# Encoder layer: four AdaLN columns on TensorE, a shorter first norm, last additions on GpSimd and TensorE, sixteen output places

## The chip, the cores and the metric

One NeuronCore of a Trainium2 chip. It has a matrix engine (TensorE: PE for products, PEld for loading their weights), a vector engine (VectorE: DVE), a scalar engine (ScalarE: ACT), a general one (GpSimd: POOL), and queues that issue DMAs (here SyncE's, SP, and a few at the end on ACT's). Products accumulate in PSUM, eight banks of 128 x 512 f32; everything else works in SBUF. The metric is the device time of one execution in microseconds.

## What is computed

One layer of an encoder on 2048 tokens of width 1024, all f32: windowed attention, then a SwiGLU feed-forward net, each with a norm before and after and with shift, scale and gate from a conditioning vector c (AdaLN).

```python
c_act = jax.nn.silu(c)
mod = (c_act @ ada_w[i] + ada_b[i])[:, None, :]
sh1, sc1, g1, sh2, sc2, g2 = jnp.split(mod, 6, axis=-1)
h = rmsnorm(x, mix_norm_pre[i]) * (1.0 + sc1) + sh1
y = windowed_gqa_sink(h, att_w_qkv[j], att_w_o[j], att_sink[j], rel_bias)
x = x + g1 * rmsnorm(y, mix_norm_post[i])
h = rmsnorm(x, ffn_norm_pre[i]) * (1.0 + sc2) + sh2
y = swiglu(h, ffn_w_in[i], ffn_w_out[i])
x = x + g2 * rmsnorm(y, ffn_norm_post[i])

def rmsnorm(x, g):
    y = xf * lax.rsqrt(jnp.mean(xf * xf, axis=-1, keepdims=True) + EPS)
    return (y * g).astype(x.dtype)
```

mod has 6 x 1024 entries. In the kernel an entry stands on a partition, so mod is 48 columns of 128: columns 0 to 7 are the first shift (sh1), 8 to 15 the first scale (sc1), and so on.

## The kernel before, in words

Activations are kept transposed: width on partitions, in KT = 8 tiles of 128, and tokens along the row, in four chunks of CH = 512. An f32 product is made of three: each operand is split into a rounded part `hi` (ACT writes it as a cast) and a rest `lo` (a subtraction on DVE or POOL), and `three` multiplies hi by hi, hi by lo and lo by hi at the fast rate. A product of two plain f32 operands, as the sums of squares against `ones`, is one call and two records in the profile.

The kernel does not run in the order in which it is written. A recorder takes down every operation, and a planner of its own (`forward`, `backward`, `schedule`) sets the order per engine from assumed costs (`cost`) and from times at which each operation is due; an addition or a scaling given to POOL may be moved to DVE. So every instruction bears one line of the helper that emits it (L748), and what names a place is the tile. Engines and queues work their lists in order. A tile's place in SBUF or PSUM is taken again when its last reader is through.

The parts that the change touches:

- **The start (chunk 0).** SP loads the eight tiles `x` of chunk 0, then c, the AdaLN weights `ada` (512 KB for a column of mod) and the projection weights `wqkv` (448 KB for a row of tiles) in turn, through five places `raws`. `squares0` squares the x tiles on ACT and adds them in pairs on DVE; `rstd_of` multiplies the sums by `ones` on PE, which leaves the mean on every partition, and makes of it a first value of the inverse root on ACT (Ln, Exp) and one Newton step (a square on ACT, three operations on DVE). `ada_reduce` multiplies a tile of ada_w by silu(c), `cb`, and sums the row on DVE: one column of mod. `Chunk.h(k)` scales x by the norm (DVE), applies scale and shift (ACT) and splits the result.
- **The first wave.** For each k, seven output tiles of the projection get their three products with `hi`, `lo` of tile k: 8 groups of 21 products, into seven PSUM banks. Afterwards come the other five output tiles, with weights `w1` (the second part of a row of wqkv, 320 KB).
- **The output projection of the attention** (`OProj.fill`): its result `y` of a chunk, eight tiles, has twelve places (four in the last chunk).
- **The end.** The last part of the feed-forward net's second product is done plainly for chunks 2 and 3, chunk 3 in two halves of 256 columns: per output tile twelve products (`gls`, `wl`), an addition into `z` on DVE, a square on ACT, an addition into `zacc` on DVE. When a section's eight tiles are through, `rstd_out` makes its norm and `finish` writes z * norm, then * gate + x (two DVE operations), and a DMA stores it. In the last half the eight squares `zsl` go to PE one by one as eight sums.

## Time and profile before

| | |
|---|---|
| Median of three runs | 2037.0 us (2036.87 to 2037.06) |
| The profiled execution | 2036.67 us, its span 2034.9 us |
| Granted clock of TensorE, mean | 0.995 |
| Busy: PE, PEld, DVE, ACT, POOL | 1991.0, 1659.3, 1703.6, 1069.9, 554.4 us |
| PE's idle time | 43.9 us of the span |
| DMA | 415.23 MB, mean 204 GB/s |

A row of a timeline is the start, the duration, the engine, the source line, the operation, its tiles and shapes, how many, and in brackets how long the engine was idle before and what released it. Durations of products overlap, so their rate is read from the distance of starts. Groups give the total and the mean duration in ns of one instruction. A row of stretches gives busy time and instructions of each engine between two times.

### The profile page before, as it was taken

To read this page: it belongs to the slowest core of one execution; us is meant where nothing else is said; L and a number is where in the kernel's file an instruction comes from. 1 tells how busy PE (TensorE), PEld (TensorE's weight loads), DVE (VectorE), ACT (ScalarE), POOL (GpSimd) and SP (SyncE) were. 2 spreads that over 40 slices of the span, in tenths; PEclk is the share of its full clock that TensorE was granted. 3 is DMA by queue.
4 is the path that set the end of the run, shared out by engine and by line. 5 is a ranking of instruction groups with operands and counts; after the bars stand their busy time and mean duration, and the time that the engine had idled before them with its cause. 6 is when DMAs were issued, how large, how long until landed. Compare 5 with 4: busy or idle time off the path is not lost.

```text
span 2034.9 us, 28945 instructions
## 1 busy us (share of the span) xinstructions
PE 1991.0 (98%) x9366; PEld 1659.3 (82%) x9366; DVE 1703.6 (84%) x3075; ACT 1069.9 (53%) x2094; POOL 554.4 (27%) x501
## 2 busy tenths in 40 slices
PE   5999999999999999999999999999999999999997
PEld 4888888888787778788888888888888888888886
DVE  7868888877989888988787998776776789989998
ACT  5557766777778864344343533333333744455432
POOL 1302342344657513432333221111111000120031
PEclk9999999999999999999999999999999999999999
DMA  8896765576787694444446743333233694398543
GB/s 308 303 324 211 241 210 173 192 279 229 253 279 251 226 361 150 160 161 166 165 160 242 272 155 130 119 135 104 83 124 105 240 334 144 117 326 297 173 154 109
DMA packets 208580, 415.23 MB, mean 204 GB/s; under 512 B 19963, under 2 KB 61996, under 8 KB 205356
## 3 DMA queue, kind: packets, MB, share of 16 engines
q1 hardware_dynamic: 207852, 412.84, 58.7%
q8 instruction: 75, 1.23, 0.2%
q14 instruction: 77, 0.63, 0.1%
q10 hardware_dynamic: 576, 0.52, 0.1%
HBM read 278.52 MB, written 134.77 MB: 203 GB/s over the span
## 4 chain that ended last, share of the span: by engine, by line
PE 91%; DVE 5%; DMA 2%; issue 1%; ACT 1%; SPq 0%; POOL 0%; DVEq 0%; ACTq 0%; POOLq 0%
PE bank L748 91%; DVE z L748 1%; DVE ada L748 1%; DVE zx L748 1%; DVE pr L748 0%; DMA o_d<-of 0%; DMA ly<-y_d 0%; DMA x<-xT 0%; DMA ol<-o_d 0%; SPq L748 0%; DVE u_i L748 0%; DMA ada<-ada_w 0%; DVE x L748 0%; DVE plo L748 0%; DVE ws_i L748 0%
## 5 line engine op out<-in xcount | busy, mean ns | idle before, releaser
L748 PE MATMUL bank<-ht,ws_i 128*128 128x512 f32 x1584 | 374.0, 389 | 0.0
L748 PEld LDWEIGHTS bank<-ht,ws_i 128*128 128x128 f32 x1584 | 297.3, 188 | 61.7
L748 PE MATMUL bank<-hb,wa_i 128*128 128x512 f32 x1056 | 254.2, 389 | 0.4 <-DVE hb L748 0.4
L748 PEld LDWEIGHTS bank<-hb,wa_i 128*128 128x128 f32 x1056 | 198.1, 188 | 42.0 <-DVE hb L748 0.7
L748 PE MATMUL bank<-ol,wo 128*128 128x512 f32 x768 | 206.1, 396 | 2.3 <-ACT yacc L748 1.1
L748 DVE TENSOR_TENSOR u_i<-bank,u_i 128x512 f32<-128x512 f32 x176 | 120.9, 688 | 80.0 <-PE bank L748 77.8
L748 ACT CAST ws_i<-s_i 128x512 fp32r<-128x512 f32 x132 | 81.9, 620 | 192.2 <-DVE s_i L748 96.2
L748 ACT ACTIVATE pr<-pr,nm 128x385 f32<-128x385 f32 (+1 forms) x256 | 154.8, 606 | 53.3 <-DVE nm L748 47.4
L748 DVE CUSTOM_DVE_ANT_0 pr<-bank,bias,nsink 128x384 f32<-128x384 f32 (+1 forms) x256 | 149.9, 594 | 25.6 <-PE bank L748 22.0
L748 PEld LDWEIGHTS bank<-ol,wo 128*128 128x128 f32 x768 | 141.2, 188 | 28.7 <-ACT yacc L748 1.5
L748 POOL TENSOR_SCALAR pr<-pr,rs 128x384 f32<-128x384 f32 (+1 forms) x177 | 114.7, 660 | 179.7 <-DVE rs L748 168.3
L748 POOL TENSOR_TENSOR p_i<-p_i,u_i 128x512 f32<-128x512 f32 x41 | 66.9, 1632 | 344.6 <-DVE u_i L748 173.9
L748 POOL TENSOR_TENSOR z<-z,z 128x512 f32<-128x512 f32 x29 | 45.4, 1577 | 345.9 <-ACT ws_o L748 264.4
L748 PE MATMUL bank<-k,q 128*128 128x384 f32 (+1 forms) x512 | 135.5, 345 | 1.5 <-DVE nm L748 1.5
L748 PE MATMUL bank<-hi,ws 128*128 128x512 f32 x384 | 134.3, 400 | 0.0
L748 DVE TENSOR_TENSOR plo<-bank,phi 128x512 fp32r<-128x512 f32 x184 | 120.8, 684 | 9.8 <-ACT phi L748 8.7
L748 PE MATMUL bank<-hb,ws_i 128*128 128x512 f32 x528 | 127.1, 390 | 1.8 <-ACT p_i L748 1.8
L748 ACT CAST wa_i<-wiri 128x512 fp32r<-128x512 f32 x132 | 81.3, 620 | 90.1 <-PE bank L748 78.4
L748 PE MATMUL bank<-ht,wa_i 128*128 128x512 f32 x528 | 126.8, 389 | 0.0
L748 DVE TENSOR_TENSOR wa_i<-wiri,wa_i 128x512 fp32r<-128x512 f32 x132 | 103.4, 784 | 19.0 <-ACT wa_i L748 19.0
L748 PEld LDWEIGHTS bank<-hb,ws_i 128*128 128x128 f32 x528 | 98.9, 188 | 23.2 <-ACT p_i L748 2.6
L748 DVE TENSOR_TENSOR z<-bank,z 128x512 f32<-128x512 f32 (+1 forms) x164 | 107.7, 659 | 11.4 <-PE bank L748 10.2
(261 smaller groups left out, 4422.6 us busy)
## 6 DMA issues: line engine op xcount, KB each, us to landing
wiri<-w_in SPq DMA_DIRECT2D x88, 512.0 KB, 4.6
ada<-ada_w SPq DMA_DIRECT2D x40, 512.0 KB, 5.1
q_d<-e SPq DMA_DIRECT2D x32, 512.0 KB, 4.4
q<-q_d SPq DMA_DIRECT2D x16, 1024.0 KB, 7.0
wo<-wo_d SPq DMA_DIRECT2D x16, 1024.0 KB, 6.0
wiro<-w_out SPq DMA_DIRECT2D x40, 384.0 KB, 5.0
g_d_b<-p_i SPq DMA_DIRECT2D x44, 256.0 KB, 3.3
g_d_t<-p_i SPq DMA_DIRECT2D x40, 256.0 KB, 2.0
```

The source lines that it names most:

```text
L748: o.ins = getattr(engs[o.eng], o.fn)(*args, **kw)
```

## The change

**AdaLN columns on TensorE.** Columns 8, 0, 9 and 1 of mod, which groups 0 and 1 need, come from PE: `ct` holds silu(c) as 128 x 8, `ada_t` holds ada_w in the orientation of a product, and `ada_products` makes eight products of 128x128 weights with one column of ct, summed in one column of a PSUM bank; DVE adds the bias. DVE's reductions of these four columns go (52 instead of 56 in all). The silu of the long `cb` now comes later.

**Norm and split at the start.** `squares0` leaves four sums instead of three with one addition less. For chunk 0, `rstd_of(short=True)` replaces the square on ACT and three DVE operations by three DVE operations. `Chunk.h` of chunk 0 writes `hi` by its own activation, next to that of x, instead of a cast of x. `WARM` = 14 products of `ones` with itself are put first on PE; nothing reads them.

**Places and splits.** AdaLN tiles of the start get ten places of their own (`raws0`) whose space w2 takes afterwards. The lo parts of the first part of wqkv go to DVE alone.

**The end.** The norm's last operation writes to PSUM (`keep`), z is scaled in one operation by gate and norm (`scaled`), and x is added on POOL (`finish_apart`; the planner leaves four to DVE). Squares are added on POOL where the planner keeps them there. In the last half, pairs of squares are added before PE sums them (five sums instead of eight), and x + z is made on PE by products with the identity, copied by ACT.

**Sixteen places** for y of the output projection instead of twelve.

The planner lays the whole order anew; its cost of a plain f32 product gets a floor of 230 ns.

```diff
+ADA_PE = 2
+WARM = 14
...
-                op.occ, op.lat = 860 * n // CH, 1060 * n // CH
+                op.occ, op.lat = max(860 * n // CH, 230), max(1060 * n // CH, 400)
...
-    def rstd_of(alloc, psp, ptag, acc, tag, r=None, direct=False):
+    def rstd_of(alloc, psp, ptag, acc, tag, r=None, direct=False, short=False, keep=False):
...
         act.activation(r, ps, AF.Ln, bias=epsc)
         act.activation(r, r, AF.Exp, scale=-0.5)
+        if short:
+            dve.scalar_tensor_tensor(t, ps, EPS, r, ALU.add, ALU.mult)
+            dve.scalar_tensor_tensor(t, t, -0.5, r, ALU.mult, ALU.mult)
+            out = ps if keep else r
+            dve.scalar_tensor_tensor(out, t, 1.5, r, ALU.add, ALU.mult)
+            return out
...
-            dve.tensor_tensor(sq[6], sq[4], sq[6], ALU.add)
-            self.acc = [sq[0], sq[2], sq[6]]
+            self.acc = sq[::2]
...
-            act.activation(xt, xt, AF.Identity, bias=mod[:, k:k + 1], scale=coef[:, 0, k:k + 1])
...
+            if c == 0:
+                act.activation(hi, xt, AF.Identity, bias=mod[:, k:k + 1], scale=coef[:, 0, k:k + 1])
+            act.activation(xt, xt, AF.Identity, bias=mod[:, k:k + 1], scale=coef[:, 0, k:k + 1])
+            if c == 0:
+                return scaled, dve.tensor_tensor(lo, xt, f(hi), ALU.subtract)
...
+        raws0 = open_pool(first, "raws0", KT * C2 * 2 // D, side="right")
...
+        sp.dma_start(ct, a["ct"])
         sp.dma_start(cb, row(a["c"], D))
...
+        def ada_products(k):
+
+            for e, t in enumerate((8 + k, k)):
+                w = raws0.tile([P, D], F32, tag="raw", name=f"adat{t}")
+                sp.dma_start(w, a["ada_t"][t])
+                j = 2 * k + e
+                for i in range(KT):
+                    pe.matmul(ada_ps[:, j:j + 1], w[:, i * P:(i + 1) * P], ct[:, i:i + 1],
+                              start=i == 0, stop=i == KT - 1)
+                dve.tensor_tensor(mod[:, t:t + 1], ada_ps[:, j:j + 1], adab[:, t:t + 1], ALU.add)
...
-            split(t[:, 0], t[:, 1], w[:, :n], pool)
+            split(t[:, 0], t[:, 1], w[:, :n], pool if i else dve)
...
+        for _ in range(WARM):
+            pe.matmul(warm[:, :P], f(ones), f(ones), start=True, stop=True)
...
-            ada_reduce(*ada_load(8 + k, raws))
-            ada_reduce(*ada_load(k, raws))
+            if k < ADA_PE:
+                ada_products(k)
+            else:
+                ada_reduce(*ada_load(8 + k, raws0))
+                ada_reduce(*ada_load(k, raws0))
...
-                y = yp.tile([P, CH], F32, tag="y", name=f"y{c}_{n}", bufs=4 if c == NCH - 1 else 12)
+                y = yp.tile([P, CH], F32, tag="y", name=f"y{c}_{n}", bufs=4 if c == NCH - 1 else 16)
...
+    def scaled(c, k, r, cols):
+        y = ys[c, k][:, cols]
+        dve.scalar_tensor_tensor(y, y, coef[:, 3, k:k + 1], r, ALU.mult, ALU.mult)
+        return y
+
+    def finish_apart(c, k, r, cols):
+        y, xr = scaled(c, k, r, cols), late_x[c, k][:, cols]
+        pool.tensor_tensor(xr, xr, y, ALU.add)
+        sp.dma_start(out[c, :, k, cols], xr)
...
-                square(c, n, cols, dve)
+                square(c, n, cols, pool)
...
+                if n % 2 and n < KT - 2:
+                    pool.tensor_tensor(sq[n - 1], sq[n - 1], sq.pop(n), ALU.add)
...
-    r = rstd_out(*prev, lsq)
+    r = rstd_out(*prev, list(sq.values()), keep=True)
+    c, cols = prev
     for k in range(KT):
-        finish(prev[0], k, r, late_x[prev[0], k], prev[1], (dve, dve))
+        xr = late_x[c, k][:, cols]
+        ps = psC.tile([P, CH], F32, tag="p", name=f"px{k}")[:, cols]
+        pe.matmul(ps, ident, xr, start=True, stop=False)
+        y = scaled(c, k, r, cols)
+        pe.matmul(ps, ident, y, start=False, stop=True)
+        act.copy(xr, ps)
+        (act if k % 2 else sp).dma_start(out[c, :, k, cols], xr)
```

What stands in a row now, at three places. A name's first number is left out; its last one only counts tiles.

**PE from its first instruction**, before (sums of squares, then group 0 of the first wave):

```order
L748 MATMUL bank<-nsq_0_86,ones 128x512
L748 MATMUL bank<-nsq_2_95,ones 128x512
L748 MATMUL bank<-nsq_6_115,ones 128x512
L748 MATMUL bank<-hi_0_164,w_0_137 128x512 x7
L748 MATMUL bank<-lo_0_176,w_0_137 128x512
L748 MATMUL bank<-hi_0_164,w_0_137 128x512
```

and after:

```order
L756 MATMUL bank<-ones 128x128 x14
L756 MATMUL bank<-nsq_0_103,ones 128x512
L756 MATMUL bank<-nsq_2_113,ones 128x512
L756 MATMUL bank<-nsq_4_122,ones 128x512
L756 MATMUL bank<-nsq_6_132,ones 128x512
L756 MATMUL bank<-ct,adat_105 128x1 x8
L756 MATMUL bank<-ct,adat_111 128x1 x8
L756 MATMUL bank<-ct,adat_120 128x1 x8
L756 MATMUL bank<-ct,adat_125 128x1 x7
L756 MATMUL bank<-hi_0_199,w_0_168 128x512 x7
L756 MATMUL bank<-lo_0_216,w_0_168 128x512
L756 MATMUL bank<-hi_0_199,w_0_168 128x512
```

The products with `ct` (one column each) stand between the sums and group 0; the eighth of the last tile comes twelve products later.

**DVE at the same place**, from the last addition of squares to the norm's last operation, before:

```order
L748 TENSOR_TENSOR nsq_6_115<-nsq_4_105,nsq_6_115 128x512
L748 ISA ada_93,mod<-ada_93,cb,adab 128x1024
L748 ISA mod 128x1
L748 ISA ada_98,mod<-ada_98,cb,adab 128x1024
L748 ISA mod 128x1
L748 TENSOR_TENSOR w_0_137<-wqkv_0_103,w_0_137 128x896
L748 SCALAR_TENSOR_TENSOR nta_143<-bank,nta_143 128x512
L748 ISA ada_113,mod<-ada_113,cb,adab 128x1024
L748 ISA mod 128x1
L748 TENSOR_SCALAR nta_143<-nta_143 128x512
L748 SCALAR_TENSOR_TENSOR coef<-mod,gains 128x1
L748 TENSOR_TENSOR nr_129<-nr_129,nta_143 128x512
```

and after, to the first `lo`:

```order
L756 TENSOR_TENSOR nsq_6_132<-nsq_6_132,nsq_7_137 128x512
L756 TENSOR_TENSOR mod<-bank,adab 128x1
L756 SCALAR_TENSOR_TENSOR nta_170<-bank,nr_148 128x512
L756 SCALAR_TENSOR_TENSOR nta_170<-nta_170,nr_148 128x512
L756 TENSOR_TENSOR mod<-bank,adab 128x1
L756 SCALAR_TENSOR_TENSOR nr_148<-nta_170,nr_148 128x512
L756 SCALAR_TENSOR_TENSOR coef<-mod,gains 128x1
L756 TENSOR_TENSOR x_0_71<-x_0_71,nr_148 128x512
L756 TENSOR_TENSOR w_0_168<-wqkv_0_115,w_0_168 128x896
L756 TENSOR_TENSOR x_1_75<-x_1_75,nr_148 128x512
L756 TENSOR_TENSOR mod<-bank,adab 128x1
L756 TENSOR_TENSOR lo_0_216<-x_0_71,hi_0_199 128x512
```

The reductions (`ISA ada`, with the readout `ISA mod`) are gone from ahead of the norm; two additions of one column take their place, and the second stands ahead of the norm's last operation.

**DVE around the lo tile of group 5**, before:

```order
L748 ISA ada_286,mod<-ada_286,cb,adab 128x1024
L748 ISA mod 128x1
L748 SCALAR_TENSOR_TENSOR coef<-mod,gains 128x1
L748 ISA ada_255,mod<-ada_255,cb,adab 128x1024
L748 ISA mod 128x1
L748 TENSOR_TENSOR lo_4_359<-x_4_76,hi_4_331 128x512
L748 ISA ada_300,mod<-ada_300,cb,adab 128x1024
L748 ISA mod 128x1
L748 TENSOR_TENSOR lo_5_371<-x_5_78,hi_5_357 128x512
```

and after:

```order
L756 ISA ada_244,mod<-ada_244,cb,adab 128x1024
L756 ISA mod 128x1
L756 ISA ada_254,mod<-ada_254,cb,adab 128x1024
L756 ISA mod 128x1
L756 SCALAR_TENSOR_TENSOR coef<-mod,gains 128x1
L756 TENSOR_TENSOR w_5_370<-wqkv_0_266,w_5_370 128x896
L756 ISA ada_280,mod<-ada_280,cb,adab 128x1024
L756 ISA mod 128x1
L756 TENSOR_TENSOR lo_5_416<-x_5_90,hi_5_397 128x512
```

Now a group's two reductions, its coef and the weights' lo come in a row, and before lo of group 5 (`lo_5`) stands one reduction of group 6.

**The end.** PE after the products of the last output tile, before:

```order
L748 MATMUL bank<-gls_3_17735,wl_17915 128x256 x3
L748 MATMUL bank<-zsl_18263,ones 128x256 x2
L748 MATMUL bank<-zsl_18273,ones 128x256 x2
L748 MATMUL bank<-zsl_18283,ones 128x256 x2
L748 MATMUL bank<-zsl_18295,ones 128x256 x2
```

after (`zsl` are the squares, `zx` the x tiles, `z` the scaled results):

```order
L756 MATMUL bank<-zsl_18233,ones 128x256
L756 MATMUL bank<-zsl_18266,ones 128x256
L756 MATMUL bank<-zsl_18292,ones 128x256
L756 MATMUL bank<-zsl_18346,ones 128x256 x2
L756 MATMUL bank<-zx_0_17857,ident 128x256
L756 MATMUL bank<-zx_1_17878,ident 128x256
L756 MATMUL bank<-zx_2_17892,ident 128x256
L756 MATMUL bank<-zx_3_18223,ident 128x256
L756 MATMUL bank<-zx_4_18250,ident 128x256
L756 MATMUL bank<-zx_5_18281,ident 128x256
L756 MATMUL bank<-z_0_6_16505,ident 128x256
L756 MATMUL bank<-z_1_6_16606,ident 128x256
```

POOL's last instructions were, before:

```order
L748 TENSOR_TENSOR z_1_4_16504<-z_1_4_16504,z_1_3_16487 128x512
L748 TENSOR_TENSOR z_2_6_16915<-z_2_6_16915,z_2_1_16608 128x512
L748 TENSOR_TENSOR z_2_4_16782<-z_2_4_16782,z_2_3_16709 128x512
L748 TENSOR_TENSOR z_3_6_16963<-z_3_6_16963,z_3_1_16643 128x512
L748 TENSOR_TENSOR z_3_4_16824<-z_3_4_16824,z_3_3_16741 128x512
```

and are, at the place that feeds PE's sum of `zacc_18076` (chunk 3's first half), after:

```order
L756 TENSOR_TENSOR zacc_17927<-zacc_17927,zsq_5_0_18028 128x512
L756 TENSOR_TENSOR zacc_18076<-zacc_18076,zsq_3_0_18130 128x256
L756 TENSOR_TENSOR zacc_18076<-zacc_18076,zsq_4_0_18142 128x256
L756 TENSOR_TENSOR zx_0_17724<-zx_0_17724,z_0_2_16407 128x512
L756 TENSOR_TENSOR zacc_18076<-zacc_18076,zsq_5_0_18159 128x256
L756 TENSOR_TENSOR zx_1_17739<-zx_1_17739,z_0_5_16441 128x512
L756 TENSOR_TENSOR zacc_18076<-zacc_18076,zsq_6_0_18201 128x256
L756 TENSOR_TENSOR zx_2_17758<-zx_2_17758,z_1_2_16559 128x512
L756 TENSOR_TENSOR zx_4_17792<-zx_4_17792,z_2_2_16707 128x512
L756 TENSOR_TENSOR zacc_18076<-zacc_18076,zsq_7_0_18215 128x256
L756 TENSOR_TENSOR zsl_18233<-zsl_18233 128x256
L756 TENSOR_TENSOR zx_7_17843<-zx_7_17843,z_3_5_16892 128x512
```

POOL gets additions of zacc, of x and of pairs of squares that DVE had or that did not exist; PE's sum of `zacc_18076` stands in its list in the sixth of the last section's eight output tiles.

## The prediction

> **What bounds the kernel now.** I read the page's engine totals first, then busy times by stretch, then PE's waits and the timeline of the first 60 us and of the last 20.

> ```profile
> span 2034.9 us, 28945 instructions
> PE 1991.0 (98%) x9366; PEld 1659.3 (82%) x9366; DVE 1703.6 (84%) x3075; ACT 1069.9 (53%) x2094; POOL 554.4 (27%) x501
> ...
> 13.57:23.70 10.13, 2.04 (x2) 0.47 (x2) 8.81 (x16) 7.06 (x9) 1.33 (x1) 1.00 0.98 370
> 23.70:47.06 23.36, 23.36 (x91) 18.73 (x91) 21.97 (x37) 11.12 (x15) 2.21 (x2) 1.00 0.91 305
> 47.06:50.28 3.22, 0.00 (x1) 0.01 (x1) 3.22 (x4) 1.57 (x2) 1.99 (x2) 0.87 0.71 225
> 50.28:57.96 7.68, 7.68 (x22) 6.09 (x22) 7.68 (x8) 3.94 (x7) 4.34 (x3) 0.61 0.88 289
> 57.96:2018.90 1960.94, 1950.38 (x9234) 1630.31 (x9233) 1645.06 (x2970) 1036.22 (x2049) 543.87 (x491) 1.00 0.58 202
> 550.00:850.00 300.00, 290.41 (x1390) 238.18 (x1390) 261.56 (x489) 198.61 (x404) 140.60 (x137) 0.99 0.71 242
> 2018.90:2022.40 3.50, 3.41 (x16) 2.65 (x14) 3.50 (x11) 0.82 (x2) 0.00 (x0) 1.00 0.15 49
> 2022.40:2034.90 12.50, 0.00 (x0) 0.00 (x0) 9.69 (x27) 1.31 (x3) 0.00 (x0) 0.63 0.45 158
> ```

> The stretch rows give start and end, length, then busy us and instructions of PE, PEld, DVE, ACT and POOL, the granted clock, the DMA share and GB/s. PE is the bound: 1950.38 of 1960.94 us between 57.96 and 2018.90, so only 10.6 us are idle there, 9.6 of them between 550 and 850. Whatever shortens the run must come from the two ends: PE's real work begins at 23.70, and after 2022.40 PE does nothing for 12.5 us. An early start is kept, since nothing else is full in the middle (DVE 1645 of 1961 us).

> ```profile
> 12.01 1.42 DVE L748 TENSOR_TENSOR nsq<-nsq,nsq 128x512 f32<-128x512 f32 x2 [0.63 <-ACT nsq L748]
> 13.28 1.06 ACT L748 ACTIVATE cb<-cb 128x1024 f32<-128x1024 f32 x1
> 13.57 2.04 PE L748 MATMUL bank<-nsq,ones 128*128 128x512 f32 x2 [1.32 <-DVE nsq L748]
> 15.65 0.69 ACT L748 ACTIVATE nr<-bank,epsc 128x512 f32<-128x512 f32 x1
> 22.19 0.81 ACT L748 ACTIVATE x<-x,mod,coef 128x512 f32<-128x512 f32 x1
> 23.70 3.35 PE L748 MATMUL bank<-hi,w 128*128 128x512 f32 x7 [8.09 <-ACT hi L748]
> ...
> 45.08 1.98 PE L748 MATMUL bank<-hi,w 128*128 128x512 f32 x8
> 50.28 0.79 PE L748 MATMUL bank<-lo,w 128*128 128x512 f32 x1 [3.22 <-DVE lo L748]
> 50.87 0.63 PE L748 MATMUL bank<-hi,w 128*128 128x512 f32 x1
> 51.29 0.63 PE L748 MATMUL bank<-lo,w 128*128 128x512 f32 x1
> ...
> 57.96 0.39 PE L748 MATMUL bank<-lo,w 128*128 128x512 f32 x1
> ```

> The first wave runs in eight groups (k) of 21 matmuls. Warm, one follows the other after (1.98 - 0.39) / 7 = 0.227 us; after the wait of 3.22 us they follow after 0.42 (50.87, 51.29), the slow rate. At 57.96 the first 112 are through (91 up to 47.06, 21 after 50.28). Without loss 112 take 25.4 us; here they took 34.3. The excess of 8.9 is one stall of 3.22 and about 5.6 of slow clock and waiting for the first lo tile. From 57.96 to the end of the attention's start PE hardly waits, so **the moment at which the 112th matmul is through** is my measure for the start.

> **The start, part by part.** The sums of squares: one of two additions in a row goes (1.42 / 2 = 0.71), the tiny transfer of ct goes ahead of x (one issue, about 0.45 by SP's spacing of x: an estimate from 3.71 us for eight). The last sum then starts at 13.57 - 0.71 + 0.45 = 13.3. In before it took 2.04 at the slow clock; WARM's fourteen products run before x arrives and the sums follow at gaps under 3 us, so I take half, 1.0: done at 14.3. Ln and Exp, 0.69 each, give 15.7; the silu table and cb (which were ahead of them on ACT) now come later. Should the clock be slow here, the sums cost 1.0 more.

> The 32 products of one column have no row. Each is two records of an f32 weight load and a minimal matmul:

> ```profile
> 300.67 0.93 PE L748 MATMUL bank<-ident,pr 128*128 128x128 f32 x7
> ...
> L748 PE MATMUL bank<-ident,pr 128*128 128x128 f32 x736 | 111.0, 273 | 2.4 <-DVE pr L748 1.2 <-POOL pr L748 1.2
> ...
> L748 PEld LDWEIGHTS bank<-nsq,ones 128*128 128x128 f32 x6 | 1.5, 310 | 12.5 <-DVE nsq L748 9.7 <-issue 2.9
> ```

> Transposes load 128x128 f32 weights every (0.93 - 0.273) / 6 = 0.11 us: the nearest row, and the low end. The high end is a load of 0.310 (the slow-clock row) plus a matmul of 0.273 in turn, 0.58. I take 0.11: 16 records, 1.8 us per ada tile. The tiles land in time: x is down at about 11.8, and 512 KB at 370 GB/s take 1.4, so they land at about 13.3, 14.7, 17.4, 18.8 with the weights between. PE does them in its queue behind the sum: 14.3 to 16.1 (column 8), 17.9 (column 0), 19.7, and seven of the last tile's eight until 21.3. Those seven stand **ahead of the first main matmul** though nothing in group 0 needs them.

> DVE: column 8's addition, two shorter norm steps (0.69 each, to 17.6), column 0's addition at 18.0, the third norm step 18.7, coef and x scaled (0.15 + 0.60) 19.5; ACT writes hi directly (0.81): 20.4. PE is free at 21.3 and starts at about 21.4, which is 2.3 earlier. On ACT the silu of cb (1.06) and its table load (some 1.3, the gap of 14.34 to 15.65 ahead of Ln) now stand before hi of group 1: ACT is through with them at 24.5, that hi is done at 25.4 and needed at 26.4. The removed hi cast (0.6) is worth something at the first group alone; later ACT has room (11 of 23 us).

> After that it is DVE against PE:

> ```profile
> 41.87 1.28 DVE L748 CUSTOM_DVE_ANT_0 ada<-ada,cb,adab 128x1024 f32<-128x1024 f32 x1
> ...
> 43.07 0.15 DVE L748 SCALAR_TENSOR_TENSOR coef<-mod,gains 128x1 f32<-128x1 f32 x1
> ...
> 46.42 3.19 DVE L748 CUSTOM_DVE_ANT_0 ada<-ada,cb,adab 128x1024 f32<-128x1024 f32 x1
> ...
> 49.54 0.68 DVE L748 TENSOR_TENSOR lo<-x,hi 128x512 fp32r<-128x512 f32 x1
> 46.44 2.08 POOL L748 TENSOR_TENSOR w<-wqkv,w 128x896 fp32r<-128x896 f32 x1 [21.15 <-DMA ada<-ada_w]
> ...
> L748 DVE TENSOR_TENSOR w<-wqkv,w 128x896 fp32r<-128x896 f32 x3 | 3.3, 1085 | 1.4 <-ACT w L748 1.4
> ```

> A group k >= 2 costs DVE two ada reductions of 1.20 (41.87 to 43.07), coef 0.07, the weights' lo of 1.08 (now all eight on DVE, four were on POOL), x and lo 0.60 each: 4.75 us. PE needs 21 x 0.227 = 4.77. Groups 0 and 1 have no reductions, which is DVE's head start. Stepped through the new order from 21.4: PE would begin groups 1 to 5 at 26.4, 31.2, 36.0, 40.8 and 45.6; DVE has lo of groups 2, 3, 4 at 30.5, 35.9, 40.7, and of group 5 at 46.1, because a third reduction stands before it. So 0.5 is lost, and the 112th matmul is through at 46.1 + 1.6 = 47.7 against 57.96. The DMA is not late: with ten more places for raw tiles a group needs 2 x 512 + 448 KB, 4.1 us at 370 GB/s.

> Two subtractions. POOL's splits of w1 now fall at the end of this wave, and the row at 46.42 shows what that does: a reduction took 3.19 instead of 1.28 while POOL ran. I charge one, 1.9 us; bounds none and five. [...]
> And the clock: a slow start costs 13 x 0.2 = 2.6, as at 50.28; PE has only one-column products in the 7 us before, so I charge half, 1.3. [...]
> Gain of the start: 57.96 - 47.7 - 1.9 - 1.3 = **7.1 us**, bounds 3 and 10.5.

> **The end.**

> ```profile
> 2018.69 3.62 PE L748 MATMUL bank<-zsl,ones 128*128 128x256 f32 x16
> 2019.56 0.42 ACT L748 ACTIVATE zsl<-z 128x256 f32<-128x256 f32 x1 [0.25 <-DVE z L748]
> 2022.69 0.47 ACT L748 ACTIVATE nrz<-bank,epsc 128x256 f32<-128x256 f32 x1 [2.72 <-DVE z L748]
> 2025.43 0.42 DVE L748 TENSOR_TENSOR nrz<-nrz,ntz 128x256 f32<-128x256 f32 x1
> 2026.24 0.67 DVE z L748 x2
> 2026.91 0.79 DVE zx L748 x2
> 2030.27 2.28 ACTq L748 DMA_DIRECT2D out<-zx  x4
> 2031.22 0.88 DVE L748 SCALAR_TENSOR_TENSOR zx<-z,coef,zx 128x256 f32<-128x256 f32 x2
> ```

> Before, eight sums of 3.62 / 8 = 0.45 follow the last product, so Ln waits until 2022.69 although the last square is there at 2019.56 + 0.42 = 2019.98. After, three of five sums are done earlier; one follows: Ln at 2020.6, two earlier. Ln, Exp and three DVE steps (0.47 + 0.42 + 3 x 0.42) replace 3.16 us, but DVE is the queue here: from 2019.5 it has eight scalings of the half before (0.40 each, from 0.79 / 2), one addition and the three steps, 4.9 us, to 2024.4, then eight more to 2027.5. PE adds x and z with f32 identity products of 0.45: from 2024.7 eight z and two late x, 4.5 us, to 2029.2; a copy on ACT (0.42) 2029.7 and one more issue, 0.35. Before, DVE's last operation ended at 2032.1. Gain 32.1 - 30.05 = **2.0 us**; bounds 3, and -2.5 if PE had gone slow and the ten products took 0.9 each, as the first sums did against the later ones. [...]

> The rest. POOL's additions (zacc, zx) feed a sum that stands in PE's queue in the sixth of the last eight groups: covered as long as POOL's chain is done by about 2015, see rival four. Sixteen places add no instruction and remove waits between chunks; no row of PE names them as releaser, and I take 0, bounds -3 and +4, as the planner also re-laid the whole order and the 10.6 us of idle time in the middle may change.

> **Sum.** The profiled execution took 2036.67 (span 2034.9 and 1.8 around it), 0.33 under the median of 2037.0. 2036.67 - 7.1 - 2.0 = 2027.6, on the median's scale **2027.9**.

> **The rivals.**
> One, slower: the one-column products do not overlap, 0.58 per record. For: they all add into one column and share nothing with the transposes but the load. Against: transposes of other rows of the same bank run at 0.11. Then PE starts at 14.3 + 62 x 0.58 = 50.3, and with a slow clock the 112th is through at 50.3 + 25.4 + 2.6 = 78.3: 20.3 lost, 2.0 won, 2055. It decides from 0.35 us per record, where the start loses 6.1 and the total 4.1.
> Two, same: the products run at half the transposes' rate and the main wave starts slow: start at 15.3 + 62 x 0.22 = 28.9, 112th at 56.9; gain 1.1 + 2.0, 2033.9.
> Three, the start moves but DVE stays the limit: all five splits of POOL hold it, 5 x 1.9 = 9.5, so 10.3 - 9.5 = 0.8 is left; with the end 2034.2. For: DVE's 4.75 against 4.77 leaves no room. Against: most splits fall behind DVE's last lo.
> Four, the end gives nothing: nine POOL additions (four of 512 columns at about 1.6, five of 256 at half) stand between the last half's squares and PE's sum, 10.4 us in some 13; held by DVE twice, they make PE wait 2 us: 2029.9.

> **How the numbers follow.** About 0.2% (4 us) is what a measurement can tell from no change: faster below 2032.9, slower above 2041.1. Main case 0.60 (2022 to 2032.9), four 0.10, two 0.10, three 0.10, one 0.05, and 0.05 for a new order that makes PE wait in the middle, half of it slower. Faster: main, four and half of three, 0.75; same: two, the rest of three and half of the last, 0.17; slower 0.08. The range reaches down to all bounds nearly kind (10.5 + 3 + 1.5: 2022) and up past two and three, 2035.

> **What would show it.** Right: the first hi product at 21 to 22, 0.227 spacing from the start, no PE wait above 2 us before 60, the 112th near 48 to 52, the last Ln about 2 us after the last product, last products at 0.45. Wrong: ada products above 0.3 us per record, spacing of 0.42 after 21, DVE reductions of 3 us before 50, a PE wait for zacc near the end, or new waits above 3 us between 550 and 850.

## The result, and the profile after

The changed kernel took 2059.0 us (median of four runs, 2057.63 to 2059.41), the kernel before 2037.0 beside it: a ratio of 1.0109, 95% interval 1.0096 to 1.0121, 22 us slower. The prediction was 2027.9, with a range of 2022 to 2035; both the time and the sign were missed. The profiled execution took 2058.84 us, at a granted clock of 0.996.

The engine totals of the kernel after (span, then busy us, share and instructions of each engine):

```profile
span 2057.1 us, 29165 instructions
PE 2038.4 (99%) x9486; PEld 1677.3 (82%) x9486; DVE 1687.8 (82%) x3043; ACT 1077.0 (52%) x2100; POOL 571.3 (28%) x523
```

PE is busy 47 us longer than before (1991.0) and idle 19 us of its span instead of 44. So the ends did get shorter, and something made the busy part longer. Busy times by stretch say where (start and end, length, busy us and instructions of PE, PEld, DVE, ACT, POOL, granted clock, DMA share, GB/s), after:

```profile
12.56:24.52 11.96, 11.46 (x64) 11.29 (x62) 4.54 (x9) 5.93 (x8) 0.00 (x0) 0.61 1.03 409
24.52:52.87 28.35, 28.35 (x115) 22.77 (x116) 25.55 (x46) 13.66 (x17) 0.00 (x0) 0.93 0.80 300
52.87:2042.85 1989.98, 1979.77 (x9234) 1629.39 (x9233) 1646.68 (x2962) 1044.94 (x2054) 565.42 (x510) 1.00 0.58 199
1600.00:2000.00 400.00, 400.00 (x1725) 323.78 (x1724) 354.21 (x608) 196.64 (x378) 46.48 (x30) 1.00 0.64 220
2042.85:2057.06 14.21, 9.34 (x43) 7.50 (x41) 8.10 (x21) 4.61 (x12) 5.13 (x7) 0.97 0.55 192
```

The 112th product of the first wave is through (the next one starts) at 52.87, where it was 57.96: 5.1 us won. After the last main product 14.2 us are left, where it was 16.0 (2018.90 to 2034.9): 1.8 won. The stretch between, with the same 9234 matmul records as before, takes 1989.98 us where it took 1960.94: 29.0 lost. The three add up to the 22.2 us by which the span grew. The 29.0 are no waiting: PE's idle time in the middle is 10.2 us (1989.98 - 1979.77) against 10.6. So the products themselves have become slower, in the mean. The same 400 us late in the run, and the same group of products, before:

```profile
1600.00:2000.00 400.00, 400.00 (x1781) 331.09 (x1780) 362.53 (x613) 194.11 (x373) 46.67 (x30) 1.00 0.62 215
...
L748 PE MATMUL bank<-ht,ws_i 128*128 128x512 f32 x1584 | 374.0, 389 | 0.0
```

and that group after (busy us, mean ns of one):

```profile
L756 PE MATMUL bank<-ht,ws_i 128*128 128x512 f32 x1584 | 378.4, 392 | 0.0
```

PE is busy for all of both windows at a granted clock of 1.00, yet 1725 matmuls fit where 1781 did: 3% fewer. This is the feed-forward net ahead of its last part: none of the parts of the change lies here.

The start of PE's list after, with the steps of the norm on DVE and the first hi on ACT:

```profile
11.59 1.12 PE L756 MATMUL bank<-nsq,ones 128*128 128x512 f32 x2 [0.17 <-DVE nsq L756]
12.56 2.06 PE L756 MATMUL bank<-ct,adat 128*128 128x1 f32 x18
14.66 0.16 DVE L756 TENSOR_TENSOR mod<-bank,adab 128x1 f32<-128x1 f32 x1 [3.12 <-PE bank L756]
14.87 4.25 PE L756 MATMUL bank<-ct,adat 128*128 128x1 f32 x20 [0.25 <-DVE mod L756]
15.45 0.69 DVE L756 SCALAR_TENSOR_TENSOR nta<-nta,nr 128x512 f32<-128x512 f32 x1
19.16 0.16 DVE L756 TENSOR_TENSOR mod<-bank,adab 128x1 f32<-128x1 f32 x1 [3.02 <-PE bank L756]
19.23 0.68 DVE L756 SCALAR_TENSOR_TENSOR nr<-nta,nr 128x512 f32<-128x512 f32 x1
19.37 5.28 PE L756 MATMUL bank<-ct,adat 128*128 128x1 f32 x24 [0.25 <-DVE mod L756]
20.68 0.81 ACT L756 ACTIVATE hi<-x,mod,coef 128x512 fp32r<-128x512 f32 x1 [5.74 <-DVE x L756]
24.52 3.33 PE L756 MATMUL bank<-hi,w 128*128 128x512 f32 x7
...
28.08 0.63 PE L756 MATMUL bank<-hi,w 128*128 128x512 f32 x1
28.50 0.51 PE L756 MATMUL bank<-lo,w 128*128 128x512 f32 x1
28.85 0.39 PE L756 MATMUL bank<-hi,w 128*128 128x512 f32 x1
29.09 0.40 PE L756 MATMUL bank<-lo,w 128*128 128x512 f32 x1
...
33.27 0.39 PE L756 MATMUL bank<-lo,w 128*128 128x512 f32 x1
33.51 0.40 PE L756 MATMUL bank<-hi,w 128*128 128x512 f32 x1
33.74 0.39 PE L756 MATMUL bank<-lo,w 128*128 128x512 f32 x1
```

The one-column products hold PE from 12.56 to 24.5, though hi is there at 20.68 + 0.81 = 21.5. The main wave begins at the slow rate (28.08 to 28.50: 0.42) until 28.85, and then runs at 0.233 to 0.235 (33.27, 33.51, 33.74), where before had 0.227 once warm. That last number is the first sign of what costs the 29 us.

The end after (`gls` with `wl` are the last main products):

```profile
2039.06 3.79 PE L756 MATMUL bank<-gls,wl 128*128 128x256 f32 x29
2042.69 2.32 PE L756 MATMUL bank<-zsl,ones 128*128 128x256 f32 x10
2045.05 0.48 ACT L756 ACTIVATE nrz<-bank,epsc 128x256 f32<-128x256 f32 x1 [1.04 <-PE bank L756]
2047.53 3.61 DVE L756 SCALAR_TENSOR_TENSOR z<-z,coef,bank 128x256 f32<-128x256 f32 x9
2052.44 0.59 PE L756 MATMUL bank<-z,ident 128*128 128x256 f32 x2
2053.55 0.65 ACT L756 COPY zx<-bank 128x256 f32<-128x256 f32 x2 [1.40 <-DMA out<-zx]
2053.96 0.82 ACTq L756 DMA_DIRECT2D out<-zx  x2
```

Ln begins 2.2 us after the last main product (2042.85 to 2045.05); before it was 3.8 (2018.90 to 2022.69). From Ln to the end of the span it is 12.0 us, and was 12.2.

### The profile page after: what moved, and what is told of

It reads as the page before. It is cut to its first block, busy times and chain, and to the rows that moved or that the text cites. A ratio compares the mean times of both kernels' runs of the same rounds, so it can differ in the third digit from the quotient of the medians.

```text
span 2057.1 us, 29165 instructions
## 1 busy us (share of the span) xinstructions
PE 2038.4 (99%) x9486; PEld 1677.3 (82%) x9486; DVE 1687.8 (82%) x3043; ACT 1077.0 (52%) x2100; POOL 571.3 (28%) x523
## 4 chain that ended last, share of the span: by engine, by line
PE 95%; DVE 2%; issue 1%; ACT 1%; DMA 1%; POOL 0%; SPq 0%; ACTq 0%; DVEq 0%; POOLq 0%
PE bank L756 95%; DVE pr L756 1%; POOL pr L756 0%; DMA ol<-o_d 0%; DVE y L756 0%; DMA x<-xT 0%; DVE plo L756 0%; SPq L756 0%; DVE of L756 0%; DVE ol L756 0%; ACT pr L756 0%; DVE wa_i L756 0%; ACT phi L756 0%; DVE ws_i L756 0%; ACT low L756 0%
## 5 line engine op out<-in xcount | busy, mean ns | idle before, releaser
L756 PE MATMUL bank<-ht,ws_i 128*128 128x512 f32 x1584 | 378.4, 392 | 0.0
L756 PEld LDWEIGHTS bank<-ol,wo 128*128 128x128 f32 x768 | 141.9, 188 | 32.1 <-DVE wo L756 2.2
L756 PEld LDWEIGHTS bank<-ht,wa_i 128*128 128x128 f32 x528 | 99.2, 188 | 23.1
```

The lines of the kernel that those rows point to most:

```text
L756: o.ins = getattr(engs[o.eng], o.fn)(*args, **kw)
```

## The experiments

**Where the 128x512 products are slow.** Taken over all rows of the trace of after, the distance from one 128x512 product to the next falls into two kinds, by where the streamed tile and the weights lie in SBUF. The kernel fills SBUF from both ends, pool by pool. On the right side the pool `constr` is opened first; it held 192 + 128 + 32 + 128 = 480 bytes per partition, and the right side's other tiles began at 229344 - 480 = 228864, a multiple of 512. The change adds `ct`, 32 bytes, to this pool, and nearly every tile on the right side, for the whole run, lies 32 bytes lower. The left side is where it was. Of the 7686 products of 128x512, 4736 take one operand from the left side and the other from the right, in before as in after; in before the two lie at the same place within 256 bytes for all 7686, in after 32 bytes apart for these 4736.

```diff
     gains = constr.tile([P, 4, KT], F32, name="gains")
+    ct = constr.tile([P, KT], F32, name="ct")
```

So theory P: a product whose streamed tile and weights lie differently within some power of two of bytes is slower. Theory M: an operand off a boundary is slower, whatever the other does. Theory W: the loss comes from the work and order that the change puts in.

The four kernels for this leave the order of all instructions as it is (in their traces PE, DVE, ACT and POOL work the same lists) and only shift one end:

```diff
 right_512 (after):       -SBUF_RIGHT = 229344   +SBUF_RIGHT = 228864
 right_64 (after):        -SBUF_RIGHT = 229344   +SBUF_RIGHT = 229312
 before_32 (before):      -SBUF_RIGHT = 229344   +SBUF_RIGHT = 229312
 left_32 (after):         -SBUF_LEFT = 1152      +SBUF_LEFT = 1184
```

> The kernel after, its order and work unchanged, with the right end of SBUF 480 bytes lower, so that with the 32 bytes of ct the tiles on the right side lie 512 bytes below their places of before. In the trace of after the first wave and the end gained (the 112th product 5.1 us earlier, the end 1.8 shorter), and the stretch between took 29.1 us more, with 128x512 products following each other after 0.233 us in many places and after 0.227 in others. Theory P, placement: the new tile ct of 32 bytes per partition moves every tile on the right side by 32 bytes, and a product whose streamed tile and weights lie differently within 64 bytes takes 233.3 instead of 227.2 ns; 4736 products of 512 columns are of that kind, 29 us. P expects 2059.0 - 29 - about 0.5 in the first wave = 2029 to 2030, and 0.227 everywhere. Theory M, misalignment: any operand off a 64-byte boundary costs, whatever the other does; here nothing is off: 2029 too. Theory W, work and order: the loss comes from what the change puts in (its new order, more products on PE, sixteen places): 2059, and products at 0.231 to 0.234 as in after.

> The kernel after, order and work unchanged, with the right end of SBUF 32 bytes lower: with ct the right side lies 64 bytes below its places of before. P and M with a period of 64 bytes: 2029 to 2030, 0.227 everywhere. Were the period longer (128 bytes or more, which the two traces cannot tell apart, since there the two sides differ by 0 or by 32), the right side would still disagree with the left one: about 2059. W: 2059.

> The kernel before, its order and work unchanged and nothing of the change in it, with the right end of SBUF 32 bytes lower. The same 4736 products as in after then have streamed tile and weights at different places within 64 bytes. P: 2037.0 + 4736 x 6.2 ns + 288 products of half the width at about half of it = 2037 + 30 = 2067, with 0.233 in the first wave where before has 0.227. M: 5872 products of 512 columns have an operand off, 36 us, 2073. W: 2037, no change.

> The kernel after, order and work unchanged, with the left end of SBUF 32 bytes higher: now the left side, too, is 32 bytes off, so that streamed tile and weights agree again within 64 bytes while both are off. P: as with the right side moved back, 2029 to 2030; if being off together costs what 855 such pairs in after show (228.7 against 227.2 ns), 11 us more, 2041 at most. M: all 7686 products of 512 columns are off, 47 us against 29: 2077. W: 2059.

Measured, with the kernel before at 2036.06 us beside them (2037.0 beside after). "Apart" is by how much the two sides differ from a multiple of 512 bytes; the last two columns are the mean distance, worked out over all pairs of neighbouring 128x512 products of the profiled run (distances above 250 ns, which are waits or the slow clock, left out), where streamed tile and weights of the first of the pair lie on the same side (left) and on different sides (streamed left, weights right; then the other way round).

| kernel | apart | us | ratio to before (95%) | same side, ns | different sides, ns |
|---|---|---|---|---|---|
| before | 0 | 2036.06 | | 226.7 | 227.7; 226.7 |
| after | 32 | 2059.0 | 1.0109 (1.0096 to 1.0121) | 227.2 | 233.0; 233.4 |
| right_512 | 0 | 2031.52 | 0.9977 (0.9967 to 0.9986) | 226.7 | 227.5; 226.7 |
| right_64 | 64 | 2056.21 | 1.0098 (1.0081 to 1.0115) | 227.5 | 231.8; 233.3 |
| before_32 | 32 | 2062.51 | 1.0133 (1.0118 to 1.0148) | 227.2 | 233.0; 233.4 |
| left_32 | 64 | 2056.74 | 1.0104 (1.0089 to 1.0119) | 227.5 | 231.7; 233.3 |

The same 400 us in before_32, a kernel in which nothing of the change is left but the shift:

```profile
1600.00:2000.00 400.00, 400.00 (x1726) 323.73 (x1725) 355.19 (x609) 197.40 (x380) 39.73 (x25) 1.00 0.64 221
```

and the middle and the same 400 us in right_512, which has the whole change but not the shift:

```profile
54.05:2017.34 1963.29, 1953.46 (x9234) 1631.09 (x9233) 1645.84 (x2965) 1045.09 (x2054) 566.06 (x510) 1.00 0.59 202
1600.00:2000.00 400.00, 400.00 (x1786) 331.22 (x1785) 357.59 (x610) 193.65 (x370) 52.16 (x34) 1.00 0.62 214
```

W falls: the loss stays when the work goes (1726 products in the window, as after's 1725) and goes when the work stays (1786). P holds for the cause: of the 29.0 us that the middle lost, 26.7 come back with the shift alone (1989.98 against 1963.29). Its size was a little high: 26.5 us for before_32 where 30 were expected. M falls by left_32 (2077 expected, 2056.7 measured): there both sides are off and the loss is no larger than in right_64, where one is. But P was wrong on the period: with a period of 64 bytes right_64 and left_32 would have been fast. In these two the tiles lie at different places and the two sides are 64 bytes apart in both; they agree within 0.6 us, and in the distances within 0.1 ns. So what counts is the difference between the sides, and its period is longer than 64.

**The period.** Two more shifts of before:

```diff
 before_128:   -SBUF_RIGHT = 229344   +SBUF_RIGHT = 229216
 before_256:   -SBUF_RIGHT = 229344   +SBUF_RIGHT = 229088
```

> The kernel before, order and work unchanged, with the right end of SBUF 128 bytes lower. With both sides congruent within 512 bytes products follow after 0.227 us (before, right_512), with the two sides 32 or 64 bytes apart after 0.233 (after, before_32, right_64, left_32). P with a period of 128 bytes: 2037, 0.227 everywhere. P with a period of 256 or 512: as before_32, 2063, 0.233 where streamed tile and weights lie on different sides.

> The kernel before, order and work unchanged, with the right end of SBUF 256 bytes lower. P with a period of 128 or 256 bytes: 2037. P with a period of 512: 2063.

before_128 took 2060.36 us (ratio 1.0119, 1.0098 to 1.0139; different sides at 232.6 and 233.1 ns), before_256 2036.86 (1.0003, 0.9992 to 1.0013; 227.8 and 226.7). With 32, 64 and 128 slow and 256 fast, the period is 256 bytes.

**The effect by itself.** A kernel of its own, with one execution, puts tiles at known places and runs nothing beside them but some additions on DVE during the first two stretches: `ma` to `mi` are streamed and `sa` to `si` are weights, a at a multiple of 256, b 32 bytes behind it, c 64, d 96, e 128, f 160, g 192, h 224, i 256.

```python
for d in STEPS:          # ma with sa ... si
    run([(0, d)])
for d in STEPS[1:]:      # mb ... mi with sa
    run([(d, 0)])
```

> A kernel of its own that computes nothing of the layer: 29 stretches of 96 products of 128x512 (fp32r), streamed tiles ma to mi and weights sa to si lying 0, 32, ... 256 bytes behind a multiple of 256, two tiles of each in turn; nothing else runs until the last three stretches, in which DVE adds tiles beside them. P with the period of 256 bytes that the runs so far point to: 0.227 us per product for ma with sa and with si, 0.233 for ma with sb to sh and for mb to mh with sa; 0.227 again for mb with sb, md with sd, me with se, 0.233 for mb with sd. If the effect needs the traffic of other engines, everything is 0.227 in the quiet stretches and 0.233 only for ma with sd, and ma with se, beside DVE. Four stretches alternate, to tell which pair it is. If a streamed tile is hindered by the loading of the next product's weights: ma-sa, ma-sd in turn 0.230 and ma-sa, md-sa in turn 0.230, ma-sa, md-sd in turn 0.233, ma-sd, md-sa in turn 0.227. If it is the product's own weights: the last two the other way round, 0.227 and 0.233.

Its timeline (start, duration, the 96 products of a stretch in one row; the next stretch starts with the next row's start):

```profile
59.34 22.55 PE L57 MATMUL bank<-ma,sb 128*128 128x512 f32 x96
104.13 22.64 PE L57 MATMUL bank<-ma,sd 128*128 128x512 f32 x96
126.61 22.47 PE L57 MATMUL bank<-ma,se 128*128 128x512 f32 x96
171.32 22.15 PE L57 MATMUL bank<-ma,sg 128*128 128x512 f32 x96
215.70 21.92 PE L57 MATMUL bank<-ma,si 128*128 128x512 f32 x96
237.46 22.57 PE L57 MATMUL bank<-mb,sa 128*128 128x512 f32 x96
259.86 22.15 PE L57 MATMUL bank<-mc,sa 128*128 128x512 f32 x96
415.69 21.95 PE L57 MATMUL bank<-mb,sb 128*128 128x512 f32 x96
437.48 21.97 PE L57 MATMUL bank<-md,sd 128*128 128x512 f32 x96
481.08 22.56 PE L57 MATMUL bank<-mb,sd 128*128 128x512 f32 x96
```

A row is 95 distances and one product of 0.39: 21.92 is (21.92 - 0.39) / 95 = 0.2266 us, 22.55 is 0.2333, 22.64 is 0.2342, 22.15 is 0.2291. Equal places give 0.2266 to 0.2272, whatever they are: mb with sb, md with sd, and a tile 256 bytes away (ma, si). All other places give 0.232 to 0.234, save one: weights 192 bytes behind the streamed tile (ma, sg, or mc, sa, which is the same difference within 256) give 0.229. At the places tried only the difference counts, and it needs no other engine. The exception shows in the whole kernel, too: in right_64 and left_32 the right side lies 64 bytes lower, so weights there are 192 behind a streamed tile on the left, and these are the fastest of the slow ones, at 231.8 and 231.7 ns. The last three stretches, meant to have DVE beside them, had not: DVE was through with its additions by 57 us and ran beside the first stretches instead, where ma with sa took about 0.227 all the same (192 products in 46.16 us; an estimate that counts twelve of them at 0.427, as at the start of before's first wave).

Which pair hinders which was asked by alternating stretches (from the first product of one stretch to the first of the next; 96 products):

```profile
547.64:570.10 22.46, 22.46 (x97) 18.03 (x96) 0.00 (x0) 0.00 (x0) 0.00 (x0) 1.00 0.00 1
570.10:592.17 22.07, 22.07 (x97) 17.99 (x96) 0.00 (x0) 0.00 (x0) 0.00 (x0) 1.00 0.00 0
```

The first is ma-sa and md-sd in turn: each product agrees with its own weights and not with the next one's, and it is slow (22.46 / 96 = 0.234). That speaks for the loading of the next weights beside the running product. The second, ma-sd and md-sa in turn, agrees with the next one's only; it should then be fast, and is halfway (0.230, single distances of 0.225 and 0.235 in turn). So the product's own weights are not free of it either; how the two share it stays open. With the places of sb to sh the products of ma took 2 to 8 ns longer each than with that of si: what a product costs depended on where its streamed tile and its weights lay to each other.

**The parts of the change, with the sides back in step.** On right_512, one constant each:

```diff
 al_ada0:        -ADA_PE = 2   +ADA_PE = 0
 al_ada1:        -ADA_PE = 2   +ADA_PE = 1
 al_y12:         -... bufs=4 if c == NCH - 1 else 16)   +... bufs=4 if c == NCH - 1 else 12)
 al_warm0:       -WARM = 14    +WARM = 0
 al_ada1_warm0:  -ADA_PE = 2   +ADA_PE = 1   -WARM = 14   +WARM = 0
```

> The kernel right_512 (the change with the right side back at its old places within 512 bytes), with ADA_PE = 0: all AdaLN columns on DVE again, no one-column products. In right_512 these products ran at 0.112 us per record for the first 18 and at 0.214 for the next 44, when the clock had fallen, and PE came free for the first main product only at 26.46. Theory S (the one-column products do not keep the clock up and hold PE and the norm back): the first main product comes at 21 to 23, four reductions of 1.2 us are back on DVE, which then is the limit of the first wave; the two nearly cancel, 2030 to 2033. Theory R (the columns on PE are what the gain at the start comes from): the 112th product falls back to about 58, 2035 to 2036.

> The kernel right_512 with ADA_PE = 1: two columns on PE (the two that the first group needs), the next two on DVE again. S: half of the one-column products go from ahead of the first main product, which comes about 4 us earlier, at 21 to 23, and the slow stretch at its start is the shorter; DVE has 2.4 us more in group 1; 2029 to 2031. R: 2033 to 2034, between right_512 (2031.5) and the old start.

> The kernel right_512 with twelve places for y instead of sixteen, as before the change. The prediction gave the sixteen places nothing (bounds -3 and +4). If that holds: 2031.5, at most 1 us either way, though the order is laid anew. If the places are what keeps PE from waiting in the attention: 2034 or more.

> The kernel right_512 without the fourteen products of ones at PE's start. Sums of squares then run at the slow rate (1.0 us instead of 0.53 to 0.74 per record pair's half, as in before), the last is done about 1 us later, and the one-column products run at 0.214 from the first on: 18 records at 0.214 instead of 0.112, 1.8 us more. So 2.8 us later at the first main product, 2034, if PE is what holds it; if it is DVE's chain and the arrival of x, 2031.5 to 2032.5.

> The kernel right_512 with both changes that helped alone: ADA_PE = 1 (2029.5) and no products of ones at the start (2027.0, the order of the rest nearly that of right_512). If both act at the same place, on the time until the first wave runs: the first main product at 20 to 21 instead of 26.46, and 2025 to 2028. If the order that the planner lays anew counts for more than the part that is changed, as the 8 us that twelve places for y cost suggest (5.4 of them before any y exists), it may be anywhere from 2025 to 2035.

Measured (before: 2036.7 beside the first two, 2036.5 beside the next two, 2036.4 beside the last); the other columns are read from the profiled runs: first main product, 112th through, and PE's idle time from there to the last main product.

| kernel | us | ratio to before (95%) | first | 112th | idle in the middle |
|---|---|---|---|---|---|
| right_512 | 2031.52 | 0.9977 (0.9967 to 0.9986) | 26.46 | 54.05 | 9.8 |
| al_ada0 | 2035.54 | 0.9996 (0.9987 to 1.0006) | 20.34 | 48.72 | 16.4 |
| al_ada1 | 2029.53 | 0.9965 (0.9952 to 0.9978) | 21.43 | 49.48 | 10.7 |
| al_y12 | 2039.66 | 1.0016 (1.0007 to 1.0026) | 26.16 | 54.37 | 16.8 |
| al_warm0 | 2027.04 | 0.9954 (0.9939 to 0.9969) | 22.31 | 50.70 | 9.4 |
| al_ada1_warm0 | 2027.89 | 0.9963 (0.9949 to 0.9977) | 22.11 | 49.42 | 11.3 |

Without one-column products the 112th product comes 5.3 us earlier than in right_512, not later: that they hold PE back, as theory S has it, holds; that DVE takes as much back within the first wave does not. R's mechanism falls, though the time is the one that R gave. The 5.3 are given back behind the first wave: 6.6 us more of waiting in the middle and an end that is 1.5 longer. The planner has laid the whole order anew, which is the likely reason, but not shown to be it. With twelve places the middle has 7.0 us more idle time, 8.1 us in all. Some 5 of the 7.0 lie between 550 and 850 us, where `y` is made: PE is busy there for 286.95 us, in right_512 for 291.96. The kernel before, with twelve places too, has 290.41, so the places alone do not explain it. So neither run prices its part: what the part does and what the new order does come together, and they are of the same size. Whether sixteen places are worth anything under an equal order was not tried. My remark in the last expectation, that 5.4 of the 8 us arise before any y exists, was read from the end of the first wave, which other products share in the two orders; the 112th product (54.05 and 54.37) shows that it was wrong.

al_warm0 is a miss of the expectation: it is 4.5 us faster than right_512 where 0 to 2.5 us slower was expected. Of these runs it is the nearest to a fair comparison, but not a clean one: besides the fourteen products that are gone, 78 of its 9458 matmul records stand elsewhere in PE's list, all of them between 163 and 211 us, and so do some operations of the other engines. Its start, where the sums are followed by the one-column products:

```profile
12.49 2.06 PE L756 MATMUL bank<-ct,adat 128*128 128x1 f32 x18
14.81 2.39 PE L756 MATMUL bank<-ct,adat 128*128 128x1 f32 x20 [0.25 <-DVE mod L756]
17.45 5.00 PE L756 MATMUL bank<-ct,adat 128*128 128x1 f32 x24 [0.25 <-DVE mod L756]
22.31 3.33 PE L756 MATMUL bank<-hi,w 128*128 128x512 f32 x7
```

The twenty records that took 4.25 in after and 4.38 in right_512 take 2.39 here: the clock falls later (the granted clock of the first 30 us is 0.83, in right_512 0.72), and 38 records run at the fast rate instead of 20. That is 2.0 us, and 0.3 more in the last group. But with one and the same order this group varies as well. In right_64, which has the order of right_512 and the fourteen products, it is

```profile
17.38 3.09 PE L756 MATMUL bank<-ct,adat 128*128 128x1 f32 x20 [0.25 <-DVE mod L756]
```

and in left_32 it took 4.43. So one profile does not show that it is the early products that make the clock fall sooner. Another 1.9 us are the start of the one-column products, 12.49 against 14.38 in right_512's profile; among the profiles with WARM it lies between 12.2 and 14.7, with the arrival of x, so it is no effect that this pair proves. And about 4 us lie in the middle, 1959.28 against 1963.29 with idle times alike. By the starts of the same product in both traces, al_warm0 is ahead by 3.4 us at 174, by 5.3 at 249, by 6.8 at 720 and by 7.4 from 1625 on. So 1.8 of the 4 arise where the two orders differ, and most of 1.5 about 710, where right_512's clock is at 0.50 from 706.3 to 709.6. The stretch of the attention's end in right_512:

```profile
550.00:850.00 300.00, 291.96 (x1392) 239.61 (x1393) 267.26 (x488) 200.31 (x406) 141.21 (x138) 0.99 0.70 244
```

and in al_warm0:

```profile
550.00:850.00 300.00, 292.70 (x1400) 240.85 (x1400) 266.71 (x480) 198.13 (x399) 140.10 (x137) 1.00 0.69 242
```

The granted clock is 0.99 in the one and 1.00 in the other; over the whole run the profiles have 0.995 and 0.997. Over the ten runs of right_512 the time goes with it, 2029.3 to 2030.3 us at 0.997 and 2032.9 to 2033.4 at 0.995. All four runs of al_warm0 had 0.997. At that clock the two are 3 us apart. Whether WARM has to do with the clock later on is open, and so is what leaving it out is worth by itself.

The two helpful edits do not add up (2027.89 for both). Both al_warm0 and al_ada1 beat the kernel before and the one after; al_warm0 is 9.4 us below the former.

## Why the prediction was wrong

- **The step that failed** is in the first paragraph and in the sum: "An early start is kept, since nothing else is full in the middle". The sum had no term for the 9234 matmul records between the start and the end; it took their rate of 0.227 us as given. The middle took 29.0 us more in place of 0, against a gain of 6.9 at both ends. The 32 bytes of ct changed the rate of 4736 products: with the sides back in step the same order took 26.7 us less in the middle and 27.5 less in all (right_512). The other 2.3 us of the middle stay open. None of the four rivals had this in it either; that rival one gave nearly the right time, 2055, is chance, as its reason was the one-column products. Of the signs that the prediction named, the spacing of 0.227 is the one that bears on this loss: it was 0.233. The profile before could not show it, as all tiles agreed within 256 bytes there; the change does add a tile to a pool at the base of one side.
- **Gain of the start**, 7.1 with bounds 3 and 10.5: measured 5.1 in after, 3.9 in right_512's profile, 7.3 in al_warm0's. The bounds held. But the sum came near by terms that were wrong in both directions, as the next points show: the first main product came 3.1 us later than forecast, and from there to the 112th product it took 28.4 us instead of 29.5.
- **The sums** were through at 12.7 instead of 14.3. In after the records of WARM follow each other after 0.213 us up to 4.84 and after 0.112 from 4.96 on, and all four sums ran at the fast rate (1.12 to 1.13 us a pair of records; without WARM, in al_warm0, the first took 2.07), and the last square was done 1.2 us sooner than before (10.81 against 11.97). That gaps under 3 us keep the rate up was the prediction's estimate: in before the second and third sum took 2.08 and 2.04 us behind gaps of 2.33 and 1.32, in after the second took 1.13 behind 1.29.
- **The one-column products** were the mis-sized term of the start: 62 records took 11.96 us in place of 6.8. The value taken, 0.11 per record, holds for the first twenty (18 in 2.06). Then the clock fell, and the rest took (5.28 - 0.35) / 23 = 0.214. This is rival two's price for two thirds of them. With the first main product at 24.52 instead of 21.4, it ate 3.1 us. Beside it, DVE's addition of column 0 stands ahead of the norm's last step and waited 3.02 us for these products (19.16); that cost nothing more here, as hi was written at 21.5 and PE came free at 24.5.
- **The clock of the main wave**: 1.3 was charged. Ten products ran at the slow rate, 4.33 us from 24.52 to 28.85 instead of 2.27: 2.1. The granted clock of 12.56 to 24.52 was 0.61 (0.99 up to 15.14 and 0.50 from there), though one-column products kept PE busy for 11.46 of these 11.96 us: here they did not keep the clock up. That they would cost half of a slow start was the prediction's estimate; of its two values, 1.3 and 2.6, the second was the nearer.
- **POOL beside DVE's reductions**: 1.9 was charged, and nothing was due. POOL starts its first split at 54.95, behind the 112th product, and all eleven reductions up to there take 1.27 to 1.29 us. PE waits for no lo tile. The 0.5 us that the prediction charged for lo of group 5 at 46.1 was not due by its own times either: five products with hi stand ahead of it, and they last until 46.7. Rival three, DVE as the limit, is out: at 0.233 and a later start PE is the slower of the two.
- **The end**: 2.0 forecast, 1.8 measured, and in the way described: Ln comes 1.6 us sooner after the last product, and the chain behind it is 0.2 shorter. The additions by PE ran without a wait above 0.85 us. Rival four did not come: PE waits for no zacc.
- **Idle time in the middle** under the new order: no term, 10.2 against 10.6. It came out right, but by luck: al_ada0 and al_y12, laid anew for one constant each, have 6 to 7 us more.
- **Without the shift** the time lies inside the range, with half of the gain: right_512 took 2031.5, 4.5 us below the kernel before where 9.1 were forecast. Its ends won 5.7 us, and its middle took 2.4 more than before's. Two profiles of the same order, before and before_256, differ by 1.6 there, so I do not explain it.

## What to carry to other kernels

Where a kernel's time is one engine's busy time, look for what can change the price of each of its instructions, not only for waits: a new tile of 32 bytes at the base of a region moves everything behind it, and 6 ns on half of the matmuls outweighed all that the change had won. Keep tiles that TensorE streams and tiles that it loads as weights at the same place within 256 bytes (0.227 us per product in the kernel rates, against 0.229 to 0.234 otherwise); here moving the base of one side did it, and padding a small constant to 256 bytes should do the same (not tried). And count the matmuls in a window that is full in both profiles and holds the same kind of work; that one number (1781 and 1725) separates a slower rate from any story about waits.
